# Attention steps taken two at a time, with TensorE held to the order in which the program names its work

## The chip, the cores and the metric

The kernel runs on one core of a Trainium2 chip. The metric is the device time of one execution in microseconds (us). TensorE (PE in the profile; PEld is its weight load) multiplies, VectorE (DVE), ScalarE (ACT) and GpSimd (POOL) work on elements, SyncE (SP) only issues DMA transfers. The five engines run their own lists of instructions, each in the order that was fixed when the kernel was built, and wait for one another by semaphores.

## The reference, cut to what matters

One layer of a model over 2048 tokens of width 1024: an input projection; a token mixer of three parts (latent attention with 8 heads, a gated delta rule with 4 heads, pooling); an output projection and a norm; a mixture of 32 experts; a last norm. The change touches the attention and the delta rule:

```
for qb in range(S // 128):                       # attention, block-causal
    s = (q_nope . k_nope + q_rope . k_rope) * scale
    p = softmax(where(k_chunk <= q_chunk, s, -inf))
    out = p @ v

def step(state, inp):                            # delta rule, 32 chunks of 64 tokens
    v_new = u_i - w_i @ state
    o_i   = q_i @ state + qk_i @ v_new
    state = state * gl_i + k_i^T @ v_new
```

## The kernel before, in words

Everything is float32 to the outside; most matrix products are made as three products of a high and a low part.

**Attention** (`attention`, L611). A unit is one head and 512 queries: 32 units, `for n, (h, cc) in enumerate(units)` (L769). A unit has `nj = 4 * cc + 4` steps of 128 keys (L803), 320 steps in all. Each step issues:

- **scores**: three products into one of three PSUM buffers, tag "st" (L809 to L811). The last four steps of a unit are on the diagonal and have 512, 384, 256 and 128 columns;
- two exponentials on ACT, a float32 one (L815) and a float16 one (L816), and their difference on DVE or POOL (L818): the high and the low part of P;
- **P times V**, at most 12 small products of 65 columns into the one buffer "pv" (L785). It is not issued in its own step: `lag.add(..., LAG)` with LAG = 4 puts it behind the scores of the step three further on. After a unit's last step `finish` (L788) divides by the sums on DVE, and for every second head `out` (L793) transposes the result through a PSUM buffer of the tag "mx" (L797) and stores it;
- one piece of the **maxima** of a unit three ahead (`max_pieces`, L688): a product into one of two PSUM buffers "mx" (L697, `MXB` = 2) and a `reduce_max` on DVE (L699), the only reader that frees the buffer. When a unit's maxima are complete, `row` (L713) multiplies once more into an "mx" buffer (L715) and ACT copies a row of it into the queries (L716).

`Lag` (L75) is a list of functions with counters; each `tick` runs those that are due.

**Delta rule** (`gdn`, L911). It is a generator that runs beside the attention. Each of its steps issues a little work and yields a price; the driver at L1991 gives it 100 for each attention step and calls it while the account is positive. Its parts are the chunk matrices (`gdn_chunks`, price RCH = 180), the inverses (`gdn_inverse`: 30 steps on POOL at RIN = 170, a pause, then small products), and the scan (`gdn_scan`, L1049, price RSC = 140). A chunk u of the scan has three steps:

- pk = keys times state (L1159), then rt from it on DVE (L1162); yield;
- pn = inverse times rt (L1167), then vn from it on ACT (L1169); transposes that prepare the next group may follow (L1100, L1105); yield;
- pd = keys times vn (L1178), then the new state S on DVE (L1182), and po, the output (L1191, L1192); transposes may follow (also L1136); yield.

All of the delta rule's PSUM tiles (pk, pn, pd, po and the transposes) share two buffers, tag "gd" (`GDB` = 2). A tile po lives from an even chunk to the end of the odd one.

**Order.** The kernel is written with a library that has a scheduler: in the version before it is free to order each engine's instructions by readiness and the order of emission, with a model of durations; the semaphores follow from the order it chose. `tc.keep_in_program_order` pins single instructions; `tc.manual_schedule` (L1939, off) would keep the order of emission.

Of the kernel before, what the change touches and what calls it, by code (L numbers as in the profile page):

```python
# [19 lines left out]
D = 1024  # L20
S = 2048
P = 128
# [4 lines left out]
C = 64  # L27
# [6 lines left out]
# experts ordered by load: blocks of 128 rows set aside for each place in that order  # L34
# [15 lines left out]
LAG = 4  # L50
# [14 lines left out]
# rows and columns at which the blocks of a chunk's matrix begin: the diagonal ones, and that above them  # L65
# [9 lines left out]
class Lag:  # L75
    """work that is issued a step after what it waits for"""
# [23 lines left out]
class Trunk:  # L100
# [22 lines left out]
    def phase_a(self):  # L123
        nc, tc, io = self.nc, self.tc, self.io
        v = nc.vector
        with ExitStack() as es:
# [20 lines left out]
            def w_split(ws, w):  # L147
                """high and low parts; of the narrow tile in one, its columns twice"""
                wH = wp.tile([P, KD, P], F32R, tag="wH", name="a_wH", bufs=3)
                if w == 3:  # L150
                    h = slice(0, 64)
                    nc.scalar.activation(wH[:, :, h], ws[:, :, h], AF.Copy)
                    pin(v.tensor_tensor(wH[:, :, 64:], ws[:, :, h], f32(wH[:, :, h]), op=ALU.subtract))
                    return wH, None
                wL = wp.tile([P, KD, P], F32R, tag="wL", name="a_wL", bufs=3)
                pin(self.split(wH, wL, ws)[1])
                return wH, wL
# [82 lines left out]
            def quarter(k):  # L240
                """the last quarter of two slices"""
# [11 lines left out]
            def sum_rows(row, sq, lhs, cc):  # L253
                """sums over channels of a tile of squares, into rows of srow"""
# [16 lines left out]
            def rows_to_cols(dst, n, then):  # L271
                """dst [128 tokens, tile, n, 2] from rows 0, 32, .. of srow, a chunk at a time"""
# [16 lines left out]
            def evac(w, cc, pt):  # L289
                """drain one [128 channels, 512 tokens] tile; returns what the tensor engine does for it later"""  # L290
# [91 lines left out]
            for n, (i, cc) in enumerate(groups):  # L382
# [26 lines left out]
                if n in (49, 51):  # L409
                    # what the up-projections begin with  # L410
# [29 lines left out]
    # one 128-wide slice of the modulation: rows of w_mod transposed against silu(c)  # L440
# [53 lines left out]
    def rows(self, ps, wk, cols, lhs, n, ptag, **kw):  # L494
        """broadcast per-token columns (token-major, n tiles) into rows of all partitions"""
# [8 lines left out]
    def phase_a2(self, es, vH, vL):  # L504
# [12 lines left out]
        def value_weights():  # L517
            """columns scaled by powers of two that keep the values within float16"""
# [92 lines left out]
    def attention(self, es, ps, vH, vL):  # L611
        nc, tc, io, c = self.nc, self.tc, self.io, self.c
        v = nc.vector
        # what the first units' maxima need, while the projections still run
        kp = es.enter_context(self.pool(name="t_k0", bufs=1))
        wq = es.enter_context(self.pool(name="t_wq", bufs=2))
        # rows of a key or query tile: 64 + 32 channels, the negated maximum, four rows that mask the diagonal
# [33 lines left out]
        def pin(i):  # L651
            # among the projections, which must not wait for what comes by way of memory
            if early:
                tc.keep_in_program_order(i)
# [68 lines left out]
        # the maximum runs ahead of the units, one piece for each of their steps  # L723
# [44 lines left out]
        nxt, owed = AHEAD, 0  # L768
        for n, (h, cc) in enumerate(units):  # L769
# [33 lines left out]
            for j in range(nj):  # L803
# [15 lines left out]
                lag.add(lambda j=j, t0=t0, pH=pH, pL=pL, f=pv_mm: f(j, t0, pH, pL), LAG)  # L819
                if j == nj - 1:  # L820
                    lag.add(finish, LAG)
# [7 lines left out]
                while owed and todo and not fresh:  # L829
                    todo.pop(0)()  # L830
                    owed -= 1
                lag.tick()
                yield
        lag.flush()

# [1 line left out]
    def gdn_gates(self, cp, ps, tag):  # L837
        """gates of the delta rule, in steps: U = (sums of log decay, beta, 1 / |k|, 1 / 8|q|), E and F products of them"""
# [40 lines left out]
        # the queries' norms wait for their outputs  # L879
# [23 lines left out]
        # the rows the scan solves for are over their keys' norms  # L903
# [7 lines left out]
    def gdn(self, es, ps):  # L911
        """all of the delta rule beside the attention: yields after how many hundredths of its steps to go on"""
# [83 lines left out]
    def gdn_inverse(self, sp, ps):  # L996
        """(1 - A) inverse of all chunks, A transposed, so upper: halves of the diagonal row by row, and what couples them"""
# [32 lines left out]
        # V12 = (V11 B12) V22, the first product transposed, of four heads at a time  # L1030
# [18 lines left out]
    def gdn_scan(self, es, ps):  # L1049
# [17 lines left out]
        def load(g):  # L1067
# [4 lines left out]
            def dma(dst, src):  # L1072
                # memory of the scan is free only once the inverses are done
# [139 lines left out]
    def phase_c(self, rp, eo):  # L1213
# [6 lines left out]
        with ExitStack() as es:  # L1220
# [72 lines left out]
            # rows of the two affine maps that follow the norm: alpha * x1 and the experts' input  # L1293
# [5 lines left out]
            # (the norm's factor comes without the square root of the width)  # L1299
# [105 lines left out]
    def first_expert(self):  # L1405
        """the expert that has most of the first half's assignments comes first, whatever the others' order"""
# [16 lines left out]
    def first_blocks(self):  # L1423
        """two blocks of the first expert, closed with what the tiles so far assign to it"""
# [70 lines left out]
    def route_tokens(self, t0, t1):  # L1495
        """choices and weights of the tokens of tiles t0 to t1, and ranks within them"""
# [47 lines left out]
        # expert number, then place: block number * 32 + expert, and row in the block  # L1544
# [12 lines left out]
        # weights  # L1557
# [10 lines left out]
    def place_tokens(self, t0, t1):  # L1568
        """table of block number and expert times row, of the tokens of tiles t0 to t1"""
# [15 lines left out]
    def token_rows(self, idx, src, tmp):  # L1585
        """row numbers from sums of token + 1: rows without a token go to the spare ones"""
# [4 lines left out]
    def routing(self):  # L1591
        """order of the experts by load, and the tokens of each block"""
# [13 lines left out]
        # rows of: place of expert e (diagonal of places), expert at place r (one-hot of places times experts)  # L1606
# [3 lines left out]
        # static block of each (block number, expert), or one that is not there  # L1610
# [25 lines left out]
    def expert_split(self, wp, w1, w2, eng=(None,)):  # L1636
        """tiles of the split weights, and the pieces of work that fill them"""
# [9 lines left out]
    def gather(self, xg, idx, n=S):  # L1647
        """rows of the tokens (of the first n) of a block; rows without a token stay as they are"""
# [5 lines left out]
    def block_weight(self, wk, xg, ex):  # L1654
        """weight of each row's token for the block's expert"""
# [59 lines left out]
    def experts(self, rp, eo, half):  # L1715
        """generator: the blocks; the first steps are placed by phase_c among the last of its own"""
# [91 lines left out]
    def overflow_tables(self, rp, wk):  # L1808
        """blocks beyond those set aside: how many each expert needs, and the place of each"""
# [30 lines left out]
        # ncap - blocks of the experts before: what takes a number of an overflow block to one within its expert  # L1840
# [55 lines left out]
    def combine(self, rp):  # L1896
        """second norm of the sums of residual and experts' rows"""
# [35 lines left out]
    def build(self, stop=None):  # L1933
        nc, tc, io = self.nc, self.tc, self.io
        self.order = (10, 8, 2, 0, 1, 9, 6, 7, 4, 5, 3, 12, 13, 11)
        with ExitStack() as es:
# [27 lines left out]
            with ExitStack() as eb:  # L1964
# [26 lines left out]
                for i, _ in enumerate(att):  # L1991
                    owed += 100
                    while owed > 0:
                        owed -= next(side, 1 << 30)
                    if i == 3:
                        nc.gpsimd.dma_start(io["s_x1"][S:].rearrange("p (a d) -> p a d", a=8),
                                            zero[:, None, :].to_broadcast([P, 8, P]))
                for _ in side:
                    pass
# [153 lines left out]
```

## Time and profile before

| what | value |
|---|---|
| runs | 1898.05, 1903.86, 1898.96 us; median 1898.96 |
| profiled execution, its span | 1905.1 us, 30525 instructions |
| TensorE busy in it | 1695.9 us (89%) |
| stretch of attention beside delta rule | 462 to 1066 us of the span |

The profile is of one execution. "Idle before" is the time an engine stood still ahead of an instruction, with the instruction on another engine that ended it. PEclk is the granted share of TensorE's full clock. Durations of matmuls overlap, since they are pipelined: what a product costs in a stream is the distance to the start of the next one.

### The profile page before, as it was taken

What the parts mean: (1) busy time and instruction counts of PE and PEld (TensorE: products, weight loads), DVE (VectorE), ACT (ScalarE), POOL (GpSimd) and SP (SyncE); (2) the same over time, 40 slices, a digit from 0 to 9 for tenths busy, and PEclk for the clock granted to TensorE, in tenths of its full rate; (3) what the DMA queues carried; (4) which work ended last, traced back from release to release, by engine and by line L of the source; (5) the groups of instructions that cost most, each with busy time, mean ns of one, the idle gap of its engine ahead of it and who ended that gap; (6) DMA issues with size and microseconds to landing.
All of it is one profiled execution on the core that took longest, in us unless ns stands there. A gap on an engine that the chain in (4) does not pass through costs nothing. (4 is left out here: it accounts for less than half of the span.)

```text
span 1905.1 us, 30525 instructions
## 1 busy us (share of the span) xinstructions
PE 1695.9 (89%) x10849; PEld 1341.0 (70%) x10849; DVE 1450.5 (76%) x2579; ACT 1019.4 (54%) x1785; POOL 792.0 (42%) x662
## 2 busy tenths in 40 slices
PE   6998999988999899999999798997689999999950
PEld 5776777666767687878777587776567788777740
DVE  7767667587878978777776387778579998988958
ACT  5522431256877787466667533233256666665737
POOL 0101126421667834344344353434424455544437
PEclk9999999999998999999999899998799999999985
DMA  9564123654432232332202643451398999999958
GB/s 350 177 200 152 67 75 119 195 171 166 119 83 65 54 71 65 95 81 79 69 26 75 206 166 134 144 189 68 126 323 249 313 306 307 310 292 306 324 123 339
DMA packets 173163, 322.71 MB, mean 169 GB/s; under 512 B 77617, under 2 KB 102737, under 8 KB 160716
## 3 DMA queue, kind: packets, MB, share of 16 engines
q1 hardware_dynamic: 151872, 261.33, 40.3%
q0 software_dynamic: 19008, 59.28, 12.3%
q8 instruction: 86, 1.41, 0.3%
q14 instruction: 69, 0.56, 0.1%
q10 hardware_dynamic: 2128, 0.13, 0.1%
HBM read 239.20 MB, written 89.01 MB: 172 GB/s over the span
## 5 line engine op out<-in xcount | busy, mean ns | idle before, releaser
L818 POOL TENSOR_TENSOR t_pL<-t_pt,t_pH 128x512 f16<-128x512 f32 (+3 forms) x153 | 158.1, 1037 | 232.6 <-ACT t_pH L816 144.7
L699 DVE TENSOR_REDUCE t_mp<-t_px 128x1 f32<-128x512 f32 (+2 forms) x320 | 190.6, 606 | 59.6 <-PE t_px L697 58.4
L815 ACT ACTIVATE t_pt<-t_stt 128x512 f32<-128x512 f32 (+1 forms) x320 | 172.1, 538 | 115.4 <-PE t_stt L811 101.4
L186 PE MATMUL a_mm<-hH,a_wH 128*128 128x512 f32 x448 | 182.6, 411 | 15.4 <-ACT hH L176 14.7
L120 DVE TENSOR_TENSOR e_w1L<-e_w,e_w1H 128x1024 fp32r<-128x1024 f32 x126 | 169.6, 1373 | 23.5 <-ACT e_w1H L119 23.4
L119 ACT ACTIVATE e_w1H<-e_w 128x1024 fp32r<-128x1024 f32 x128 | 133.1, 1063 | 85.0 <-PE b_pg L1680 65.3
L186 PE MATMUL a_mm<-hL,a_wH 128*128 128x512 f32 x448 | 171.8, 399 | 0.1
L816 ACT ACTIVATE t_pH<-t_stt 128x512 f16<-128x512 f32 (+1 forms) x320 | 171.5, 536 | 0.1
L186 PE MATMUL a_mm<-hH,a_wL 128*128 128x512 f32 x416 | 164.9, 399 | 2.2 <-DVE a_wL L120 2.2
L785 PEld LDWEIGHTS <-t_pH 128*128 128x128 f16 x2176 | 120.5, 99 | 59.6 <-issue 46.9
L1712 POOL DMA_INDIRECT s_x<-b_yo,q_idx x47 | 80.0, 1702 | 192.8 <-DMA s_x<-b_yo,q_idx 86.5
L1680 PE MATMUL b_pg<-e_w1H,b_xH 128*128 128x512 f32 x376 | 155.4, 413 | 0.5 <-ACT b_xH L119 0.5
L809 PE MATMUL t_stt<-qH,kH 96*128 96x512 f32 (+2 forms) x320 | 145.8, 456 | 7.2 <-ACT t_pH L816 7.2
L1680 PE MATMUL b_pg<-e_w1H,b_xL 128*128 128x512 f32 x376 | 151.5, 403 | 0.0
L1680 PE MATMUL b_pg<-e_w1L,b_xH 128*128 128x512 f32 x376 | 150.5, 400 | 0.0
L818 DVE TENSOR_TENSOR t_pL<-t_pt,t_pH 128x512 f16<-128x512 f32 (+3 forms) x167 | 121.0, 726 | 35.7 <-ACT t_pH L816 34.7
L785 PE MATMUL t_pv<-vH,t_pH 128*128 128x65 f16 x1088 | 138.1, 198 | 2.6 <-DVE t_yt L791 2.6
L785 PE MATMUL t_pv<-vH,t_pL 128*128 128x65 f16 x1088 | 134.8, 196 | 1.2 <-DVE t_pL L818 0.8
L697 PE MATMUL t_px<-kH,qH 96*128 96x512 f32 (+2 forms) x320 | 122.9, 393 | 13.0 <-DVE t_mp L699 11.0
L785 PE MATMUL t_pv<-vL,t_pH 128*128 128x65 f16 x1088 | 133.2, 194 | 0.0
L810 PE MATMUL t_stt<-qL,kH 96*128 96x512 f32 (+1 forms) x320 | 121.4, 379 | 0.0
L811 PE MATMUL t_stt<-qH,kL 97*128 97x512 f32 (+1 forms) x320 | 120.9, 378 | 0.0
(489 smaller groups left out, 4789.7 us busy)
## 6 DMA issues: line engine op xcount, KB each, us to landing
e_w<-moe_w SPq DMA_DIRECT2D x96, 1024.0 KB, 9.0
m_w<-w_modT SPq DMA_DIRECT2D x48, 512.0 KB, 4.4
c_xs<-x SPq DMA_DIRECT2D x16, 512.0 KB, 4.3
c_ys<-s_y SPq DMA_DIRECT2D x16, 512.0 KB, 5.0
s_h<-c_h SPq DMA_DIRECT2D x16, 512.0 KB, 2.6
s_x<-c_r SPq DMA_DIRECT2D x16, 512.0 KB, 2.6
f_x<-s_x SPq DMA_DIRECT2D x16, 512.0 KB, 10.1
out_dram<-f_x SPq DMA_DIRECT2D x16, 512.0 KB, 4.9
```

The source lines that it names most:

```text
L119: return (self.nc.scalar.activation(hi, src, AF.Copy), (eng or self.nc.vector).tensor_tensor(lo, src, f32(hi) if hi.dtype == F32R else hi, ...
L120: (eng or self.nc.vector).tensor_tensor(lo, src, f32(hi) if hi.dtype == F32R else hi, op=ALU.subtract))
L186: nc.tensor.matmul(pt, a[:, k, :], b[k][:, cc * CH:(cc + 1) * CH], start=k == 0 and n == 0, stop=k == KD - 1 and n == len(ops) - 1)
L697: pin(nc.tensor.matmul(px[:, 0:w], qH[0:r, t * P:(t + 1) * P], kH[e][0:r, kb * CH:kb * CH + w], start=True, stop=True))
L699: pin(v.reduce_max(mp[:, t, kb:kb + 1], px[:, 0:w], axis=AX.X))
L785: nc.tensor.matmul(pv[:, t, :], a[:, ts_], b[:, j, h, :], start=j == 0 and t == 0 and i == 0, stop=j == nj - 1 and t == 3 and i == 2, skip ...
L809: nc.tensor.matmul(st[:, off:], kH[e][0:r, js], qH[0:r, off:], start=True, stop=False)
L810: nc.tensor.matmul(st[:, off:], kH[e][0:96, js], qL[0:96, off:], start=False, stop=False)
L815: nc.scalar.activation(pt[:, off:], st[:, off:], AF.Exp, scale=SCALE)
L816: nc.scalar.activation(pH[:, off:], st[:, off:], AF.Exp, scale=SCALE)
L818: eng.tensor_tensor(pL[:, off:], pt[:, off:], pH[:, off:], op=ALU.subtract)
L1680: nc.tensor.matmul(pg, a[:, k], b[:, k], start=k == 0 and i == 0, stop=k == KD - 1 and i == 2)
```

## The change

The steps of the attention are grouped in pairs. Each step still issues its scores, exponentials and difference as before; the pieces of the maxima, the ticks of `lag` and the delta rule come only after the second step of a pair, with two pieces, two ticks and an account of 200. P times V goes to a list of its own, `half`, which is ticked twice after the yield, so behind the delta rule's work: two steps' P times V stand together, behind the scores of the next pair. The loop is put under `tc.manual_schedule` for TensorE, which then keeps the order of emission; the other engines are still ordered by the scheduler.

Besides, comments are removed all over the file.

```
         nxt, owed = AHEAD, 0
+        half = Lag()
         for n, (h, cc) in enumerate(units):
...
-                lag.add(lambda j=j, t0=t0, pH=pH, pL=pL, f=pv_mm: f(j, t0, pH, pL), LAG)
+                half.add(lambda j=j, t0=t0, pH=pH, pL=pL, f=pv_mm: f(j, t0, pH, pL), LAG)
                 if j == nj - 1:
-                    lag.add(finish, LAG)
+                    half.add(finish, LAG)
                 owed += 1
...
-                while owed and todo and not fresh:
-                    todo.pop(0)()
-                    owed -= 1
-                lag.tick()
-                yield
+                if j % 2:
+
+                    while owed and todo and not fresh:
+                        todo.pop(0)()
+                        owed -= 1
+                    for _ in range(2):
+                        lag.tick()
+                    yield
+                    for _ in range(2):
+                        half.tick()
+        half.flush()
         lag.flush()
...
                 side = self.gdn(es2, pg)
                 owed = 0
-                for i, _ in enumerate(att):
-                    owed += 100
-                    while owed > 0:
-                        owed -= next(side, 1 << 30)
-                    if i == 3:
-                        nc.gpsimd.dma_start(io["s_x1"][S:].rearrange("p (a d) -> p a d", a=8),
-                                            zero[:, None, :].to_broadcast([P, 8, P]))
-                for _ in side:
-                    pass
+                with tc.manual_schedule(engines={nc.tensor.engine}):
+                    for i, _ in enumerate(att):
+                        owed += 200
+                        while owed > 0:
+                            owed -= next(side, 1 << 30)
+                        if i == 3:
+                            nc.gpsimd.dma_start(io["s_x1"][S:].rearrange("p (a d) -> p a d", a=8),
+                                                zero[:, None, :].to_broadcast([P, 8, P]))
+                    for _ in side:
+                        pass
```

## Rows read from the trace of the kernel before

**Rows 1.** The page: span, and busy time of each engine.
```profile
span 1905.1 us, 30525 instructions
...
PE 1695.9 (89%) x10849; PEld 1341.0 (70%) x10849; DVE 1450.5 (76%) x2579; ACT 1019.4 (54%) x1785; POOL 792.0 (42%) x662
```

**Rows 2.** Windows by stage: stretch, length, busy by engine, PEclk, DMA share, GB/s.
```profile
462.00:590.00 128.00, 115.50 (x1043) 87.01 (x1041) 97.85 (x173) 101.83 (x198) 73.52 (x64) 0.95 0.40 112
590.00:662.00 72.00, 62.45 (x607) 47.24 (x607) 67.24 (x109) 51.07 (x115) 66.35 (x62) 0.88 0.15 35
...
765.00:1040.00 275.00, 264.95 (x2649) 215.12 (x2648) 201.06 (x455) 164.42 (x351) 112.36 (x104) 0.99 0.25 72
1040.00:1066.00 26.00, 24.81 (x324) 18.77 (x324) 11.85 (x19) 23.03 (x49) 14.36 (x15) 1.00 0.26 93
```

**Rows 3.** Waits of TensorE, 765 to 1040 us: total us, times, longest.
```profile
PE n_ptv L1105 <- DVE n_S L1182: 4.3, 4, 1.7
PE t_px L697 <- DVE t_mp L699: 2.2, 4, 1.2
PE t_px L715 <- POOL t_dg L707: 1.3, 1, 1.3
PE t_pv L785 <- DVE t_yt L791: 1.0, 1, 1.0
PE n_po L1191 <- DVE n_kd L1101: 0.4, 2, 0.3
PE n_ptk L1100 <- ACT n_vn L1169: 0.4, 1, 0.4
PE t_pv L785 <- POOL t_pL L818: 0.3, 1, 0.3
```

**Rows 4.** Groups by form, TensorE, 462 to 1066 us: busy us, mean ns.
```profile
L809 PE MATMUL t_stt<-qH,kH 96*128 96x512 f32 x192 | 94.3, 491 | 2.6 <-ACT t_pH L816 2.6
L810 PE MATMUL t_stt<-qL,kH 96*128 96x512 f32 x224 | 92.0, 411 | 0.0
L811 PE MATMUL t_stt<-qH,kL 97*128 97x512 f32 x224 | 91.7, 409 | 0.0
```

**Rows 5.** Timeline 800 to 812 us, one maximum: start us, us, instruction.
```profile
804.18 0.40 PE L697 MATMUL t_px<-kH,qH 96*128 96x512 f32 x1
804.43 0.21 PE L785 MATMUL t_pv<-vH,t_pH 128*128 128x65 f16 x1
...
804.62 0.69 DVE L699 TENSOR_REDUCE t_mp<-t_px 128x1 f32<-128x512 f32 x1 [0.55 <-PE t_px L697]
```

**Rows 6.** The same timeline, the scan's three links (pd to S, pk to rt, pn to vn).
```profile
800.76 0.71 PE L1178 MATMUL n_pd<-n_vn,n_kd 128*128 128x128 f32 x4
...
801.41 0.43 PE L1191 MATMUL n_po<-n_S,n_qd 128*64 128x128 f32 x2
...
801.83 0.59 DVE L1182 SCALAR_TENSOR_TENSOR n_S<-n_S,g_E,n_pd 128x128 f32<-128x128 f32 x2
...
808.19 0.69 PE L1159 MATMUL n_pk<-n_S,n_k 128*128 128x128 f32 x4
...
808.63 0.48 PE L809 MATMUL t_stt<-qH,kH 96*128 96x512 f32 x1
...
809.21 0.60 DVE L1162 SCALAR_TENSOR_TENSOR n_rt<-n_pk,g_E,n_vb 128x128 f32<-128x128 f32 x2
...
809.77 0.69 PE L1167 MATMUL n_pn<-n_rt,n_u 128*128 128x128 f32 x4
...
810.29 0.60 PE L1100 MATMUL n_ptk<-consts,n_k 128*128 128x128 f32 x4
...
810.65 0.39 ACT L1169 ACTIVATE n_vn<-n_pn 128x256 f32<-128x256 f32 x1
```

**Rows 7.** Groups by line of the whole span (the page): exponentials and difference.
```profile
L815 ACT ACTIVATE t_pt<-t_stt 128x512 f32<-128x512 f32 (+1 forms) x320 | 172.1, 538 | 115.4 <-PE t_stt L811 101.4
L818 POOL TENSOR_TENSOR t_pL<-t_pt,t_pH 128x512 f16<-128x512 f32 (+3 forms) x153 | 158.1, 1037 | 232.6 <-ACT t_pH L816 144.7
```

## The prediction

> **What bounds the kernel now.** I read the page first: TensorE is busy for 89% of a span of 1905.1 us, more than any other engine [rows 1]. Its shares are averages over the span, so I cut the stretch that the change touches, 462 to 1066 us, into the delta rule's stages [rows 2]: chunk matrices to 590, inverses to 662, the scan from 765 to 1040, and a tail of attention alone. In the scan TensorE works for 264.95 of 275 us at a granted clock of 0.99, DVE for 201, ACT for 164, POOL for 112: this stage goes as fast as TensorE's queue, and its whole idle time is 10 us. In the inverses DVE has 67.24 of 72 us and TensorE 62.45, so DVE bounds there. Then the waits of TensorE in the scan [rows 3]: seven kinds, 9.9 us together, none over 1.7 us. These are the delta rule's transposes waiting for S or vn (a "gd" buffer not yet read), maxima waiting for an earlier `reduce_max` (an "mx" buffer), and little else. So the scheduler of before finds something else for TensorE to do nearly each time a result is still on its way. What is left to gain is small: these 10 us, and the price of changing over from P times V.
>
> **The parts.** The number of products, exponentials and transfers stays. What changes is TensorE's order, so each term counts changeovers or waits. I took the counts from the code, by following the counters through 160 pairs.
>
> *Fewer changeovers: -13 us.* The first product of a step's scores (L809) lasts 491 ns on average, the second and third 411 and 409, at the same 512 columns [rows 4]. The first is the one that follows other work, mostly P times V; 80 ns is the price of that entry. Today nearly each of 320 steps pays it; in pairs 160 do: 160 x 80 ns = 12.8 us. Bounds: -13, and -26 if the entries into maxima and delta rule behind P times V, now also spared, were as many again. The Trainium skill, "TensorE: Matmul & The Clock Gate", section "Step-by-step: what each phase is for", says that TensorE pulls a weight load ahead of running products, so that the next tile's weights load meanwhile. By that an entry would cost nothing, the term would be 0 and the sum below 13 us worse; the 491 against 411 ns speaks against it here, so the measurement stays.
>
> *A third "mx" buffer asked for in one pair: +22 us.* Two maxima now stand back to back and take both "mx" buffers. `row` (29 times) and `out` (15 times) are ticked right behind them, and need a third. In the stream one maximum's product takes 0.25 us (804.18 to 804.43), and its reduction ends 1.13 us after the product began (805.31) [rows 5]. With both products done after 0.50 us, `row` waits 0.63 us more, with everything behind it on TensorE: delta rule, P times V, the next scores. Nine of the 44 fall into the inverses, where TensorE has slack: 35 x 0.63 = 22 us. Bounds: 0 (the reduction were early), and 44 x 1.32 = 58 us, if DVE has another reduction of 0.69 us to do first. I take 0.63, since DVE is idle for a quarter of the scan.
>
> *Two linked steps of the scan in one pair: +16 us.* At 200 per pair and 140 per step, 28 pairs hold two consecutive steps, and the second needs the first's result. Today scores or P times V stand between them; now these are queued behind the second, and ACT waits for the scores. Pk to pn (9 pairs): pk's place ends at 808.63, pn starts at 809.77: 1.14 us. Pn to vn (9): 810.29 to 811.04, 0.75 us. Pd to S (10): pd's two calls take 0.45 us like the others' (808.19 to 808.63), so end near 801.2; S ends at 802.42; of these 1.2 us po, four calls or 0.9 us, covers all but 0.3 [rows 6]. Sum 9 x 1.14 + 9 x 0.75 + 10 x 0.3 = 20 us. Seven of these pairs have a `row` or `out` too, whose wait gives ACT and DVE time: -4, so 16. Bounds: 0, and 39 us with a reduction of 0.69 us ahead in each.
>
> *"gd" buffers within one step: +15 us.* In seven of the eight groups of the scan three steps put transposes behind pn or pd while po holds the other buffer; they wait until ACT has read pn or DVE has read pd. This is the wait that the trace already has: 4.3 us in 4, and 0.4 us in 1 [rows 3]. Midway, 0.74 us x 21 = 15 us. Bounds 0 and 21 x 1.08 = 23.
>
> *Waits of before that go: -10 us.* The waits in the scan [rows 3] belong to the old order; the new order's are counted above.
>
> *Entries at nothing.* P times V of a pair comes behind the next pair's scores; for odd steps that is one step sooner than now. After a pair's scores ACT has about two more exponentials of 0.54 us and POOL one difference of 1.04 us to do [rows 7], about 2.2 us; two maxima, the delta rule, another P times V and six products of scores lie before it, over 3 us. In the last dozen pairs maxima and delta rule are done and the cover is only some 2.2 us; if it is short by 0.4 us each, 5 us. The stage of the chunk matrices has no link inside a pair; the products of the inverses are independent. On SP and POOL the transfers keep their order and only move by a step; the DMA share of 0.25 in the scan [rows 2] leaves room. In the inverses DVE keeps the pace and has the same work.
>
> *Sum:* -13 + 22 + 16 + 15 - 10 = +30 us against the profiled execution, 1905.1 to 1935 us. Its span is 6 us above the median of 1898.96, so on the runs' scale 1929 us. Its own range, with the terms part way to their bounds and moving together: 1908 to 1950.
>
> **The rivals.**
>
> *Faster: the spacing is enough.* DVE and ACT answer before TensorE needs them, because the scheduler, knowing TensorE's fixed order, puts rt, vn and the reductions first on their queues. Then only -13 and -10 remain: 1876 us. For it: DVE and ACT are idle for 27% and 40% of the scan [rows 2]. Against: the links of 0.75 to 1.14 us are latency, not queueing; DVE began rt as its queue allowed and still took 0.60 us for it. The point that decides: 35 + 28 + 21 = 84 places against 23 us gained, so 0.27 us a place. My terms average 0.63.
>
> *Slower still: the clock falls.* In the inverses TensorE stands idle for 9.6 of 72 us and the granted clock is 0.88, a mix of its levels of 1.2 and 2.4 GHz; in the scan, with 10 of 275 idle, it is 0.99 [rows 2]. If 50 us of short waits bring the scan to 0.88 too, its 275 us become 275 x 0.99 / 0.88 = 309: +34, so 1963 us. The Trainium skill, same page, section "A second HAM failure mode: psum-queue depth-cycling", tells of a kernel whose short pauses between groups of products, from cycling through PSUM buffers, made the clock swing between its two levels. By that this rival would hold; the trace agrees only in the inverses, and the chunk stage, idle for 12.5 of 128 us, still has 0.95, so I give it little.
>
> *No change:* waits of 0.27 us a place cancel the gain, 1899 us; or the change doesn't do what it says, and the scheduler's order on TensorE hardly differs.
>
> **How the numbers follow.** Chances: the forecast 0.48, the clock 0.14, the faster rival 0.28, cancelled 0.07, without effect 0.03. A measurement here tells 0.3%, about 6 us, from no change. So faster 0.28, same 0.10, slower 0.62. The range reaches from 1876, the faster rival's middle (half of it, 0.14, is left out), to 1965, just past the clock rival (0.06 left out). The likeliest case alone has 1908 to 1950, and both signs hold much of the chance.
>
> **What would show it.** Right: L809's mean falls from 491 towards 450 ns; L715 and L797 wait for the reductions L699 some 40 times; L1167 waits for rt L1162, L1178 for vn L1169, and transposes for S or vn, some 50 us in all; the scan is longer with TensorE's share at 85 to 90%; the inverses are unchanged. Wrong: TensorE's idle time in the scan does not grow above its 10 us (the faster rival), or the granted clock of the scan drops well below 0.95 (the clock rival), or DVE or ACT goes over 90% there.

## The result and the profile after

| | before | after |
|---|---|---|
| median of the runs (range) | 1901.41 us (1898.05 to 1903.86) | 2007.16 us (2001.75 to 2016.15) |
| ratio, 95% interval | | 1.0569 [1.0534, 1.0603] |
| profiled execution, its span | 1905.1 us | 2009.1 us |

The kernel is slower, as forecast, but by 106 us and not by 30: the time lies 42 us above the end of the range. In the code after, lines stand a little lower: the scores are L810 to L812, P times V L786, the exponentials L816 and L817, the difference L819, pk L1166, rt L1169, pn L1174, vn L1176, pd L1185, S L1189, po L1198 and L1199, the transposes L1107, L1112 and L1143; the maxima stay L697 and L699, `row` L715, `out` L798.

The page after: the counts of TensorE, DVE and ACT are within a few instructions of [rows 1], so no work was added.

```profile
PE 1716.0 (85%) x10849; PEld 1380.5 (69%) x10849; DVE 1449.9 (72%) x2581; ACT 1011.4 (50%) x1785; POOL 786.4 (39%) x660
```

Windows by stage, with the columns of [rows 2]: chunk matrices, inverses, the scan (from its first to its last po), and the whole stretch.

```profile
462.00:600.00 138.00, 117.56 (x1056) 92.48 (x1055) 104.07 (x176) 102.54 (x201) 73.88 (x65) 0.90 0.38 105
600.00:667.00 67.00, 50.69 (x477) 39.40 (x474) 57.57 (x91) 39.58 (x89) 62.31 (x62) 0.88 0.15 37
...
783.00:1126.00 343.00, 285.25 (x2643) 242.57 (x2643) 203.44 (x457) 159.93 (x357) 110.89 (x102) 0.92 0.19 50
...
462.00:1175.00 713.00, 593.28 (x5689) 491.14 (x5687) 464.27 (x899) 414.73 (x880) 305.80 (x283) 0.91 0.24 66
...
872.00:875.00 3.00, 3.00 (x17) 2.53 (x16) 1.21 (x3) 0.49 (x1) 0.00 (x0) 0.50 0.17 40
...
877.00:880.00 3.00, 2.02 (x11) 1.33 (x8) 3.00 (x7) 2.18 (x5) 1.91 (x2) 1.00 0.00 0
```

The same two windows before, the whole stretch and the scan from its first po to its last:

```profile
462.00:1066.00 604.00, 568.71 (x5691) 449.75 (x5689) 458.05 (x899) 422.35 (x881) 308.63 (x285) 0.97 0.28 77
...
765.00:1015.00 250.00, 242.79 (x2415) 198.58 (x2414) 182.58 (x419) 145.93 (x313) 99.85 (x93) 0.99 0.25 68
```

TensorE's idle time is the length less the busy time: 35 us before, 120 after. So of the 109 us that the stretch grew, 84 are idle time and 25 are busy time of the same 5690 products. The last two rows of the view after, two short stretches of the scan, belong to the timeline below. DVE, ACT and POOL have the same work as before and lower shares: none of them became the bound. The scan alone went from 7 us idle to 58, and from a clock of 0.99 to 0.92.

The waits of TensorE in the whole stretch (total us, times, longest), to be held against [rows 3]:

```profile
PE t_px L715 <- DVE t_mp L699: 21.6, 17, 4.3
PE n_pn L1174 <- DVE n_rt L1169: 14.0, 9, 2.1
PE n_ptk L1107 <- DMA n_k<-s_g: 12.0, 1, 12.0
PE t_px L715 <- POOL t_dg L707: 9.6, 8, 3.4
PE t_px L715 <- ACT t_dg L711: 7.7, 5, 1.9
...
PE t_px L697 <- ACT qH L119: 6.9, 2, 6.4
PE t_py L798 <- DVE t_mp L699: 6.1, 12, 0.8
PE n_pd L1185 <- ACT n_vn L1176: 5.5, 8, 1.1
PE n_ptk L1107 <- ACT n_vn L1176: 4.8, 7, 1.2
PE n_ptv L1112 <- DVE n_S L1189: 4.1, 4, 2.0
PE n_pr L1143 <- ACT n_ot L1201: 3.3, 7, 0.5
```

L715 and L798 wait for reductions 29 times (the prediction said some 40), for 0.96 us on average; in [rows 3] neither did (1.6 us over the whole stretch before). pn waits for rt nine times, once for each of the nine pairs that the prediction counted. Beside these stand three things that it did not price: `row`'s own operand dg (POOL and ACT), the scan's first load, and the queries qH.

Twelve microseconds of the scan in a timeline (start us, us, instruction, idle time before it), with a `row` at 880.29:

```profile
869.47 0.69 PE L1198 MATMUL n_po<-n_S,n_qd 128*64 128x128 f32 x2 [2.18 <-DVE n_kd L1108]
...
873.36 0.63 PE L811 MATMUL t_stt<-qL,kH 96*128 96x512 f32 x1
...
876.20 0.19 PE L786 MATMUL t_pv<-vH,t_pH 128*128 128x65 f16 x1
...
876.92 0.48 PE L810 MATMUL t_stt<-qH,kH 96*128 96x512 f32 x1
...
877.24 0.40 PE L811 MATMUL t_stt<-qL,kH 96*128 96x512 f32 x1
...
878.06 1.49 DVE L120 TENSOR_TENSOR kL<-t_ks,kH 64x512 fp32r<-64x512 f32 x1
...
878.40 0.62 PE L697 MATMUL t_px<-kH,qH 96*128 96x512 f32 x2
...
879.47 1.27 DVE L699 TENSOR_REDUCE t_mp<-t_px 128x1 f32<-128x512 f32 x2
...
880.29 0.47 PE L715 MATMUL t_px<-t_dg,t_sel 128*128 128x512 f32 x1 [1.27 <-DVE t_mp L699]
880.60 0.61 PE L1174 MATMUL n_pn<-n_rt,n_u 128*128 128x128 f32 x4
...
881.85 1.03 PE L1107 MATMUL n_ptk<-consts,n_k 128*128 128x128 f32 x4 [0.64 <-ACT n_vn L1176]
```

Two maxima stand back to back at 878.40. DVE splits keys until about 879.5 and then reduces both; TensorE stands for 1.27 us ahead of `row`, which wants a third buffer, and again for 0.64 us ahead of transposes, which want pn read by ACT. The pn in between does not wait: while TensorE stood at `row`, rt was long made. This is the mechanism as predicted, with DVE's other work making the first wait twice the assumed 0.63 us.

The clock shows in the same place. After the pause of 2.18 us the product L811 lasts 0.63 us, and four microseconds later the same product 0.40 us: the granted clock is 0.50 from 872 to 875 and 1.00 from 877 to 880, the levels of 1.2 and 2.4 GHz. Over the whole stretch the clock stood at 0.50 for 123 us after and 34 us before; the sums of these parts, first after, then before:

```profile
sum 123.00, PE 102.03 PEld 84.46 DVE 49.37 ACT 40.28 POOL 33.55; mean PE 5.10 PEld 4.22 DVE 2.47 ACT 2.01 POOL 1.68
...
sum 34.00, PE 29.87 PEld 24.47 DVE 25.65 ACT 24.85 POOL 19.14; mean PE 4.27 PEld 3.50 DVE 3.66 ACT 3.55 POOL 2.73
```

TensorE was at work there for 102 us after and 30 us before. If its products take twice as long at half the clock, 51 and 15 us of that are lost, so the clock accounts for about 36 us (an estimate).

### The profile page after: what moved, and what is told of

It reads as the page before. It is cut to its first block, busy times and chain, and to the rows that moved or that the text cites. A ratio compares the mean times of both kernels' runs of the same rounds, so it can differ in the third digit from the quotient of the medians.

```text
span 2009.1 us, 30507 instructions
## 1 busy us (share of the span) xinstructions
PE 1716.0 (85%) x10849; PEld 1380.5 (69%) x10849; DVE 1449.9 (72%) x2581; ACT 1011.4 (50%) x1785; POOL 786.4 (39%) x660
## 5 line engine op out<-in xcount | busy, mean ns | idle before, releaser
L819 POOL TENSOR_TENSOR t_pL<-t_pt,t_pH 128x512 f16<-128x512 f32 (+3 forms) x151 | 157.4, 1049 | 335.3 <-ACT t_pH L817 211.3
L816 ACT ACTIVATE t_pt<-t_stt 128x512 f32<-128x512 f32 (+1 forms) x320 | 171.6, 536 | 221.5 <-PE t_stt L812 216.0
L699 DVE TENSOR_REDUCE t_mp<-t_px 128x1 f32<-128x512 f32 (+2 forms) x320 | 186.8, 604 | 126.8 <-PE t_px L697 125.6
L120 DVE TENSOR_TENSOR e_w1L<-e_w,e_w1H 128x1024 fp32r<-128x1024 f32 x126 | 172.0, 1391 | 23.1 <-ACT e_w1H L119 22.9
L817 ACT ACTIVATE t_pH<-t_stt 128x512 f16<-128x512 f32 (+1 forms) x320 | 172.6, 539 | 0.0
L819 DVE TENSOR_TENSOR t_pL<-t_pt,t_pH 128x512 f16<-128x512 f32 (+3 forms) x169 | 127.6, 759 | 40.0 <-ACT t_pH L817 38.7
L810 PE MATMUL t_stt<-qH,kH 96*128 96x512 f32 (+2 forms) x320 | 137.8, 431 | 0.6 <-ACT t_pH L817 0.5
L786 PEld LDWEIGHTS <-t_pH 128*128 128x128 f16 x2176 | 123.7, 102 | 18.8 <-issue 12.8
L786 PE MATMUL t_pv<-vH,t_pH 128*128 128x65 f16 x1088 | 126.6, 200 | 2.3 <-DVE t_yt L792 2.3
L786 PE MATMUL t_pv<-vH,t_pL 128*128 128x65 f16 x1088 | 125.9, 200 | 1.6 <-POOL t_pL L819 1.6
L786 PE MATMUL t_pv<-vL,t_pH 128*128 128x65 f16 x1088 | 125.3, 199 | 0.0
L811 PE MATMUL t_stt<-qL,kH 96*128 96x512 f32 (+1 forms) x320 | 123.9, 387 | 0.0
L812 PE MATMUL t_stt<-qH,kL 97*128 97x512 f32 (+1 forms) x320 | 123.4, 386 | 0.0
L1287 PE MATMUL c_pp<-c_wH,c_yH 128*128 128x512 f32 x256 | 106.6, 418 | 10.2 <-ACT c_yH L119 10.2
```

Of the source, the lines that this page charges most:

```text
L120: (eng or self.nc.vector).tensor_tensor(lo, src, f32(hi) if hi.dtype == F32R else hi, op=ALU.subtract))
L699: pin(v.reduce_max(mp[:, t, kb:kb + 1], px[:, 0:w], axis=AX.X))
L786: nc.tensor.matmul(pv[:, t, :], a[:, ts_], b[:, j, h, :], start=j == 0 and t == 0 and i == 0, stop=j == nj - 1 and t == 3 and i == 2, skip ...
L810: nc.tensor.matmul(st[:, off:], kH[e][0:r, js], qH[0:r, off:], start=True, stop=False)
L811: nc.tensor.matmul(st[:, off:], kH[e][0:96, js], qL[0:96, off:], start=False, stop=False)
L812: nc.tensor.matmul(st[:, off:], kL[e][0:97, js], qH[0:97, off:], start=False, stop=True)
```

## The experiments

The theory at this point: the fixed order is the cause, since it leaves TensorE behind the results of other engines at places that can be named, and the clock falls because of these pauses. The rivals: pairing itself is to blame, in whatever order; or the clock fell for a reason of its own. Below, "idle" is TensorE's over the stretch of attention beside delta rule, "scan" the time from the first po to the last. Outside the stretch the profiled executions take 1289 to 1304 us, though no edit is meant for them, so a difference of medians of up to 15 us need not come from the stretch.

| kernel | median us | ratio to before [95%] | stretch | idle | scan, idle, clock |
|---|---|---|---|---|---|
| before | 1901 | | 604 | 35 | 250, 7, 0.99 |
| after | 2007.16 | 1.0569 [1.0534, 1.0603] | 713 | 120 | 343, 58, 0.92 |
| e1 pairs, free order | 1900.36 | 1.0002 [0.998, 1.0025] | 603 | 41 | 250, 8, 1.00 |
| e2 single steps, fixed | 1952.89 | 1.0263 [1.0226, 1.03] | 649 | 71 | 290, 23, 0.98 |
| e3 rows late | 1968.75 | 1.0345 [1.0293, 1.0396] | 671 | 93 | 316, 44, 0.95 |
| e4 links apart | 1975.2 | 1.039 [1.0354, 1.0425] | 679 | 108 | 310, 42, 0.97 |
| e5 rows and links spread | 1939.17 | 1.0202 [1.0141, 1.0263] | 642 | 72 | 285, 22, 0.98 |
| e6 three mx buffers | 1978.19 | 1.0414 [1.0357, 1.0471] | 682 | 104 | 319, 49, 0.96 |
| e7 `START` 1000 | 1982.34 | 1.0424 [1.037, 1.0478] | 694 | 110 | 326, 52, 0.96 |
| after, once more | 2016.81 | 1.0604 [1.0555, 1.0653] | 716 | 118 | 344, 58, 0.92 |
| e8 load apart | 2005.06 | 1.0526 [1.0481, 1.0571] | 708 | 115 | 337, 56, 0.94 |
| e9 = e5, load apart | 1934.13 | 1.0165 [1.0131, 1.02] | 637 | 73 | 286, 26, 0.99 |
| e10 = e9, three gd buffers | 1911.85 | 1.0055 [1.0032, 1.0079] | 616 | 51 | 264, 7, 1.00 |
| e11 = e1, three gd buffers | 1908.82 | 1.0028 [1.0007, 1.0049] | 610 | 42 | 251, 6, 0.99 |

**e1: pairs, but TensorE's order left to the scheduler.**

```
-                with tc.manual_schedule(engines={nc.tensor.engine}):
+                with ExitStack():
```

> The changed kernel with the fixed order taken away: pairs in the same emission, but the scheduler orders TensorE as before. Theory A (the fixed order puts waits at the head of TensorE's queue; pairing by itself costs nothing): back to the level of the kernel before, 1885 to 1920 us, TensorE's waits in the attention back from about 100 us to 35 or so. Rival R1 (the pairing costs: maxima and delta rule come in bursts and later): stays above 1960 us.

The time of before came back. Windows of the whole stretch and of the scan:

```profile
458.00:1061.00 603.00, 562.13 (x5689) 463.83 (x5688) 461.82 (x900) 413.72 (x880) 314.45 (x283) 0.97 0.29 78
...
762.00:1012.00 250.00, 242.02 (x2413) 204.80 (x2412) 180.96 (x422) 142.02 (x316) 98.33 (x93) 1.00 0.25 67
```

The group of the first product of the scores (busy us, mean ns, idle before) shows the saving that the change was to bring:

```profile
L810 PE MATMUL t_stt<-qH,kH 96*128 96x512 f32 x192 | 85.6, 446 | 0.1
```

At the clock of before, the first product of the scores fell from 491 [rows 4] to 446 ns, against 407 for the product behind it: 39 ns left of 80. TensorE's busy time fell by 568.7 - 562.1 = 6.6 us, its idle time grew by 5.6, and the sum is next to zero. Pairing as emitted costs nothing and brings nothing; but the free scheduler also undid part of the pairs (233 separate runs of P times V, against 326 before and 159 after), so this is pairing as far as the scheduler kept it.

**e2: the steps of before, TensorE in the order of emission.** The driver's loop of the kernel before, put under the change's one line:

```
+                with tc.manual_schedule(engines={nc.tensor.engine}):
                     for i, _ in enumerate(att):
                         owed += 100
```

> The kernel before, single steps, with TensorE held to the order of emission. Theory A: slower than before, since results wait at the head of the queue here too, but less than in pairs, because scores or P times V stand between any two linked steps of the delta rule and a row stands behind one maximum, not two: 1915 to 1965 us, few waits of pn for rt, more changeovers (mean of the first product of scores near 490 ns). Rival R1 (pairing costs, not the order): 1895 to 1910 us.

The fixed order alone costs 2.6%, without any pair, as expected; the first product of the scores came to 513 ns and not some 490. Its waits are of other kinds: P times V for the DVE that empties "pv", and the scan's load; pn hardly waits for rt (1.3 us in 3), since other work stands between the links.

```profile
PE t_pv L785 <- DVE t_yt L791: 15.2, 12, 2.3
PE n_ptk L1100 <- DMA n_k<-s_g: 13.4, 2, 11.1
```

With e1 this makes a square (medians against before): pairs in free order +0 us, fixed order with single steps +52, both together +106. The pairs cost only where the order is fixed, and there as much again.

**e3: `row` and `out` behind P times V.**

```
-                    lag.add(out, 2)
+                    lag.add(out, 4)
...
-                    for _ in range(2):
-                        lag.tick()
                     yield
                     for _ in range(2):
                         half.tick()
+                    for _ in range(2):
+                        lag.tick()
```

> The changed kernel with row and out (the third mx buffer of a pair) ticked behind P times V instead of right behind the two maxima. Theory A: the waits of the row and of out's transposes for the reductions (21.6 + 6.1 us in the changed kernel) and of the row for its own operand dg (9.6 + 7.7 us) shrink to under 10 us; with some clock that comes back 2007 - 40 = 1967, range 1945 to 1980 us. Rival R2 (most of the loss is a lower clock or bursts, these waits only move): above 1990 us, the same idle time under other names.

The wait for the reductions is gone (1.7 us at L715 and 0.6 at L798, against 21.6 and 6.1 in the kernel after), that for dg is 11.0 instead of 17.3, and the links stay. The time lies in the expected range; the waits named there came to 13 us, not under 10. Idle time fell by 27 us and the time by 38; the scan's clock rose to 0.95.

```profile
PE n_pn L1174 <- DVE n_rt L1169: 14.6, 9, 2.1
...
PE t_px L715 <- DVE t_mp L699: 1.7, 1, 1.7
```

**e4: the delta rule's two steps of a pair on either side of P times V.**

```
                     for _ in range(2):
                         half.tick()
+                    yield
...
-                        owed += 200
+                        owed += 100
```

> The changed kernel with the delta rule served twice a pair, 100 before P times V and 100 behind it, so that no two linked steps of the scan stand side by side. Theory A: the waits of pn for rt, pd for vn and pk for S (14.0 + 5.5 + 2.1 us) shrink to under 6 us, and 2007 - 16 = 1991, with clock down to 1975: range 1970 to 1995 us. Rival R2: no change, 2000 to 2012 us. A third outcome: more changeovers, since P times V is now followed by the delta rule's products: up to 8 us of the gain given back.

Only half a hit: the time came as expected, the waits did not. The links' waits fell from 14.0 and 5.5 us to 7.8 and 1.3, not to nothing: a pair's P times V that stands between them is over in some 0.7 us (876.20 to 876.92 in the timeline above), too short a cover for a link of 1.56 us. The reductions, untouched, still cost the same (22.9 us at L715). Idle time fell by 12 us and the time by 32; busy time in the stretch fell by 22, with the scan's clock at 0.97 instead of 0.92.

```profile
PE n_pn L1175 <- DVE n_rt L1170: 7.8, 8, 1.5
```

**e6: a third "mx" buffer, paid for with one of the scores' three.**

```
-STB = 3
-MXB = 2
+STB = 2
+MXB = 3
```

> The changed kernel with one PSUM buffer moved from scores to maxima (mx 3, st 2); order and emission unchanged. If the third mx buffer is what row and out wait for, the waits of L715 and of out's transposes for the reductions (27.7 us) fall below 5 us, those of the row for its operand dg stay or grow (17 us, up to 30). But the scores then wait for the exponentials, since two of st are filled by one pair: 5 to 30 us. Net: 1980 to 2010 us. Rival: the waits for reductions stay, since DVE is late with all of them.

L715 and L798 no longer wait for a reduction at all, so it was the buffer. But a `row` that is let through at once finds its operand late: dg's waits grow from 17.3 to 24.3 us, and the scores, with a buffer less, wait 3.6 us for ACT instead of 0.5, less than expected. The time lies 2 us under the expected range.

```profile
PE t_px L715 <- ACT t_dg L711: 13.3, 6, 4.0
...
PE t_px L715 <- POOL t_dg L707: 11.0, 13, 3.1
```

**e7 and e8: the scan's first load.** In e7 the pause that the delta rule keeps ahead of its scan is longer (`START` 400 to 1000). In e8 six empty turns stand between the first load and the transposes that read it:

```
+        for _ in range(6):
+            yield
```

> The changed kernel with 600 more of pause between the inverses and the scan (three pairs). Theory A: the single wait of the scan's first transposes for the load of the keys (12.0 us) goes and 2007 falls by 10 to 16 us, to 1991 to 1997. Rival: the load's transfers are issued later too, the wait only moves: 2002 to 2010 us.

> The changed kernel with the pause put where it acts: six empty steps of the scan between the issue of the first group's loads and the first transposes of its keys (the earlier pause stood ahead of the issue). The wait of 12 us for the load goes, and about as much as a clock that falls during it: 2007 falls to 1985 to 1996 us. The 600 of pause ahead of the issue gave 1982 with the wait still there; if that gain was only from which steps share a pair, this kernel gives 1982 to 2007 without the wait, and waits of pn and pd change in number.

Both missed: the wait stayed, at 12.3 us in e7 and 10.6 in e8. A timeline of the kernel after tells what the wait is made of:

```profile
751.09 0.40 PE L697 MATMUL t_px<-kH,qH 101*128 101x128 f32 x2
...
756.46 0.64 SPq L1081 DMA_DIRECT2D n_k<-s_g  x1
...
760.88 0.58 SPq L1081 DMA_DIRECT2D n_k<-s_g  x1
...
763.46 0.88 PE L1107 MATMUL n_ptk<-consts,n_k 128*128 128x128 f32 x3 [11.97 <-DMA n_k<-s_g]
```

TensorE reached the transposes at 751.5 us, five microseconds before the first load was even issued, and started 2.6 us after the second, the last that it needs for them. From first load to transposes it is 7.0 us here and 6.8 us before (742.1 to 748.9), where TensorE had other work for that time and waited 0.2 us. What SP itself waited for, in the kernel after:

```profile
SPq L1054 <- ACT g_v L1047: 14.5, 1, 14.5
...
SPq L1081 <- DVE n_k L1066: 3.7, 1, 3.7
```

The loads stand on SP behind a store that waited for ACT, and then for DVE to clear the tile that they fill. In e8 they moved along with the transposes, to 771.9 us, SP waiting 8.7 us for that clearing. So a pause in the order of emission did not bring the load ahead of its readers; what would was not found. That e7 was nevertheless 25 us faster than the change is not explained. Its stretch is 19 us shorter, half of it idle time, half busy time at a higher clock: `row` waits 16.7 us for reductions instead of 21.6 and 12.5 for dg instead of 17.3, pn 11.3 for rt instead of 14.0, `out` 10.1 instead of 6.1. A later start also changes which delta rule steps share a pair with a `row`; whether that is the reason, no run tells.

**The change once more, unaltered.**

> The changed kernel once more, unaltered, for its clock. If the granted clock is set by the order of work, the scan shows 0.92 plus or minus 0.01 again, and about 58 us idle. If it is chance of an execution, the scan shows 0.95 to 0.97 at the same idle time, and the execution is some 10 to 15 us shorter than 2009 us.

The scan took 344 us, at 0.92 again: the clock belongs to this order of work and not to one execution. The places tell the same. In the kernel after the clock falls to 0.50 in twelve stretches of the scan; in the repeat, whose scan begins 7 us later, it falls again at eleven of these places. One of them, after and in the repeat:

```profile
810.50:813.50 3.00, 3.00 (x28) 2.75 (x28) 0.00 (x0) 0.38 (x1) 0.00 (x0) 0.50 0.54 151
...
817.50:820.50 3.00, 3.00 (x27) 2.65 (x27) 0.00 (x0) 0.38 (x1) 0.00 (x0) 0.50 0.54 148
```

**e5, e9, e10: the remedies together.** e5 has e3's order, the delta rule served after each step (also between the two scores of a pair), queries prepared earlier, and e7's start:

```
-                if len(todo) <= 3 and nxt < len(units) and nxt <= n + AHEAD:
+                if len(todo) <= 5 and nxt < len(units) and nxt <= n + AHEAD:
...
+                else:
+                    yield
```

(and e3's edit, and 100 in place of 200 as in e4)

> All remedies together in the changed kernel, order still fixed: row and out behind P times V, the delta rule served once after each step of a pair (one step between the two steps' scores, one before P times V), 600 more of pause before the scan, next unit's queries two pieces earlier. Theory A: the waits for mx, dg, rt, vn, S and the scan's first load (about 45 + 22 + 12 of 119.5 us idle) go, idle time in the attention down to 40 to 60 us, and with it the clock lost (61 us summed as 1 minus the granted share) to 20 to 35 us: 1900 to 1930 us. If the clock does not follow the idle time (R2): 1935 to 1960 us at the same idle time. A version that beats the kernel before would need idle time below 40 us, less likely.

It came out above what was expected, with 72 us of idle time and not 40 to 60, since the load's wait (13.8 us) and those for "gd" buffers remained. e9 is e5 with e8's pause in place of e7's start; e10 is e9 with `GDB` 3 and `STB` 2.

> The spread kernel (1939 us, idle 71.5 us) with that pause instead of the one ahead of the loads: its wait of 13.8 us goes, idle 55 to 62 us, 1939 - 14 = 1925, range 1915 to 1930 us. Rival: the wait is taken by something else at the same place, 1932 to 1942 us.

> The same with one PSUM buffer moved from scores to the delta rule (gd 3, st 2). Theory A: the waits of transposes for S, vn and ot (7.0 + 4.8 + 1.4 us and some) are for the gd buffer that po holds, so they fall below 4 us; scores wait a few us more for exponentials. 1925 - 8 = 1917, range 1900 to 1925 us. Rival: the transposes wait for data of their own, the waits stay at 10 us or more.

e9 missed: the load's wait is still 10.4 us, its idle time is that of e5, and 1934 us lies in its rival's range. e10 came out as expected. Waits of e9 for "gd" buffers, first, and the window of the scan of e10, where they are gone:

```profile
PE n_ptv L1114 <- DVE n_S L1193: 12.2, 6, 3.7
...
PE n_ptk L1109 <- ACT n_vn L1180: 5.5, 7, 1.1
```

```profile
771.00:1035.00 264.00, 256.74 (x2622) 220.41 (x2621) 199.64 (x452) 162.64 (x354) 111.05 (x100) 1.00 0.24 66
```

The third term of the prediction is thereby shown too: with these 17.7 us of waits gone, idle time fell by 22 us in all and the time by 22. The scan's clock, 0.99 in e9, had nothing more to give back. TensorE is idle for 7 us of e10's scan, as in the kernel before, and the clock is 1.00. The largest of what is left of its 51 idle us are the load (10.5), `row` for reductions (7.0) and the scores' missing buffer (L810 for L817, 6.6).

**e11: e1 with three "gd" buffers.**

> Pairs with TensorE's order left to the scheduler (1900 us, 40 us idle), and one PSUM buffer moved from scores to the delta rule. If the buffer that po holds still costs something when the scheduler may go round it, the waits of transposes for S (3.4 us) go and 1890 to 1897 us come out, a version under both kernels. Rival: with two buffers the scores wait for exponentials (the free order relies on three), 1898 to 1915 us.

The rival came true, a little slower than before, but not by its reason alone: the scores with two buffers wait 10.5 us for ACT, against 5.2 in e1, yet idle time is nearly that of e1, 42 against 40 us. The rest of the 8 us is busy time in the stretch, 568.5 against 561.6 us, in part at a lower clock (0.96 against 0.97). None of these versions beats the kernel before.

## Why the prediction was right and wrong

The direction and its cause held: it is the waits behind results that are on their way, of the three kinds named (69 waits, where 84 were counted). The size failed in two steps, and one reason given against the faster rival was wrong.

| term | predicted us | measured us |
|---|---|---|
| changeovers | -13 | -6.6 (busy time, e1 against before, part of the pairs kept); about -11 after (estimate below) |
| third "mx" buffer in a pair | +22 | 21.6 + 6.1 = 27.7 |
| two linked steps in a pair | +16 | 14.0 + 5.5 + 2.1 (pk for S) = 21.6 |
| "gd" buffers | +15 | 4.8 + 5.2 + 3.3 + 0.5 = 13.8 |
| dg, the scan's load, the queries | 0 | 17.3 + 12.0 + 6.9 = 36.2 |
| waits of before, and those after that no row above has | -10 | -35.3 + 4.9 (operands kd and vb) + 15.7 (the rest) = -14.7 |
| busy time by a lower clock | 0 | about 36 (estimate above) |

The rows close: 63.1 + 36.2 us of named waits and the -14.7 make 84.6 us more of idle time, and 24.6 us more of busy time make the 109 us by which the stretch grew. Of the busy time, the clock's 36 us would leave -11 for fewer changeovers.

*The three waits* came to 63 us against 53: 69 waits of 0.91 us, where 84 of 0.63 were assumed; 0.27 was the point at which the faster rival would decide. That rival had it that the scheduler puts rt, vn and the reductions first on the queues of DVE and ACT. Against it the prediction said that the links are "latency, not queueing", and for those through DVE that was wrong. pn waits 1.56 us at a link (14.0 in 9), not 1.14 [rows 6], and in all nine rt begins only when DVE ends another instruction, 0.3 to 1.5 us after pk's last product (0.98 on average); from there to pn it is 0.58. One of the nine:

```profile
818.73 0.61 PE L1166 MATMUL n_pk<-n_S,n_k 128*128 128x128 f32 x4
...
820.23 0.68 DVE L819 TENSOR_TENSOR t_pL<-t_pt,t_pH 128x512 f16<-128x512 f32 x1
...
820.83 0.61 DVE L1169 SCALAR_TENSOR_TENSOR n_rt<-n_pk,g_E,n_vb 128x128 f32<-128x128 f32 x2
821.24 0.49 PE L1174 MATMUL n_pn<-n_rt,n_u 128*128 128x128 f32 x2 [1.90 <-DVE n_rt L1169]
```

The 1.14 us held such a wait already: a reduction of 0.68 us began on DVE at 808.62, and rt behind it at 809.21. So idle shares of 27% and 40% did not help, because the one result that was wanted stood behind other work; at 878 us it was a split of keys of 1.49 us.

*"Entries at nothing" was the first step that failed.* It said that the transfers on SP "keep their order and only move by a step", and looked at `row`'s buffer but not at its other operand. In the pairs a `row` comes one pair after the last maximum, and DVE, POOL and ACT have to make dg from it in that time: 17.3 us, against 2.5 + 0.7 over the same stretch before; in free order with pairs (e1) it is already 9.8, in fixed order with single steps (e2) 2.5. The free scheduler had also hidden the way of a load from SP's queue to TensorE, 7 us, behind other work; that cover went with the fixed order, and e2 shows it without any pair (13.4 us for the load, 5.5 for the queries). The prediction asked what hides each cost only for the parts that the diff moves, and the line that fixes the order moves everything.

*"The clock falls" was the second: it was put as a rival to the sum, at a chance of 0.14, and not as a term in it.* It holds together with the waits. Over the stretch it is the estimate of 36 us above. In the scan the cost can be read between two kernels in fixed order whose scans issue nearly the same products: after, 2643 of them, 285.25 us at 0.92; e10, 2622, 256.74 us at 1.00. That is 28 us of busy time. TensorE worked for 51 us of the scan after at 0.50, and for under 2 in e10's, so the clock accounts for some 25 of the 28. The rest of the 79 us between the scans, 343 against 264, is idle time: 58 against 7. The rival had 0.88 in the scan and 34 us. With 36 us for the clock, 33 for the three entries (36.2 less the 3.4 that dg and the load cost before) and 10 for the sizes of the three waits, 1929 would have been 2008, against 2007 measured. It closes so well because the changeovers were read as what the clock's estimate leaves; the two shares are not shown apart.

In the Trainium skill, "TensorE: Matmul & The Clock Gate", the section "A second HAM failure mode: psum-queue depth-cycling" tells of short pauses between groups of products that make the clock swing between its levels. The traces agree: the scan goes from 0.99 with 7 us of waits to 0.92 with 58 us in waits of 3.3 us at most. The scans of the table fall into three groups: 1.00 to 0.98 up to 26 us of idle time, 0.97 to 0.94 at 42 to 56, 0.92 at 58; within a group the order is loose (0.95 at 44 us, 0.96 at 52). That the pauses cause it is what the runs say as far as they go, since every edit that took waits away brought the scan's clock up and the unaltered repeat did not and lost it at the same places; pauses and clock were not varied apart from one another, so the cause stays inferred.

*Fewer changeovers* was about right: in e1 the first product is 39 ns dearer than the next one, so half of 80 went, as forecast, and about -11 us is left for it after. That is an estimate; no run has the pairs whole without the waits. In the kernel after the mean is 475 ns, above the "towards 450" of the prediction; the next product is slower there too, by 13 ns against e1, the first by 29:

```profile
L811 PE MATMUL t_stt<-qL,kH 96*128 96x512 f32 x224 | 94.0, 420 | 0.0
...
L810 PE MATMUL t_stt<-qH,kH 96*128 96x512 f32 x192 | 91.1, 475 | 0.0
```

*What would show it:* the waits appeared where named, some 68 us with the operands kd and vb that the transposes make (5 us, uncounted); TensorE's share in the scan fell to 285.25 of 343, 83%, just under the 85 to 90% foretold. Its sign of being wrong for the clock, a scan well below 0.95, came too. "Inverses are unchanged" and "the chunk stage at nothing" did not hold: the first 138 us have 20 us of idle time at a clock of 0.90, where 128 us had 12.5 at 0.95, and the inverses 16 in 67 us, where they had 9.6 in 72 [rows 2]. *P times V's spacing*, entered at nothing, was right: L786 waits 1.6 us in all for POOL's difference.

## What to carry to other kernels

Where an engine's order is fixed by hand, every instruction that stands on its queue needs an answer to "who makes its operands, who frees its buffer, and what stands between", the loads and small operands too; here a link through DVE asked for about 1.5 us of other work in between, two thirds of it because DVE was at something else, and what the scheduler had hidden before was as large as what the edit moved. Count the buffers that one group of emission asks for, not those of a step. And when tens of microseconds of short waits are added to TensorE, put a lower clock into the sum as a term: here it was about a third of the loss.

## What was not expected of the hardware

The clock's share: against e10's scan, that of the kernel after has 51 us of waits more, none over 3.3 us, and 28 us more of busy time for the same products, so that a microsecond of wait cost about one and a half. On the way back, e4 took away 12 us of idle time and gained 32 in all, e3 27 and 38. From e9 to e10, where the scan's clock was already 0.99, 22 us of idle time gave only 22. And a load's way to TensorE was 7 us, before and after alike, although a transfer of this line lands 1.7 to 3.7 us after its issue (median 2.5): 4.4 us of the 7 lie between the issue of the first head's load and the second's, behind other loads on SP's queue and, after, a wait of 1.4 us for DVE to clear one of their tiles.
